# Hybrid trunk on one core: kept weights moved among the pooled branch's products, and the pool's first banks taken from other pairs

## The chip, the core and the metric

One Trainium2 chip, one core of it. The metric is the device time of one execution in microseconds; the figure for a kernel is the median over its runs. Within a trace, times count from the first instruction (the span), and the profiled execution's own time is the span and what lies around it.

## The reference, cut to what matters

```python
D_MODEL = 1024; SEQ = 1024; N_META = 16; DEPTH = 1; D_FF = 2816; HGRN_HEADS = 4; CHUNK = 64
...
h = jnp.concatenate([meta, x], axis=1)                      # 1040 rows
u = rmsnorm(h, mix_norm_pre[l])
proj = u @ w_in[l]
q, f_logit, i_in, g_out, v_pool, gate_a, gate_b = jnp.split(proj, cuts, axis=-1)
a = hgrn2(q, f_logit, i_in, g_out, lbs[l], hgrn_out_norm[l])      # 4 heads, chunked recurrence
p = multiscale_pool(v_pool, pool_proj[l], pool_scale[l])
z = (jax.nn.sigmoid(gate_a.astype(jnp.float32)) * (a @ w_branch_hgrn[l])
     + jax.nn.sigmoid(gate_b.astype(jnp.float32)) * (p @ w_branch_pool[l]))
h = h + rmsnorm(z @ w_out[l], mix_norm_post[l])
u = rmsnorm(h, ffn_norm_pre[l])
gt = causal_dwconv(u @ ffn_w_gate[l], ffn_conv_w[l], ffn_conv_b[l])
y = (jax.nn.gelu(gt, approximate=True) * (u @ ffn_w_up[l])) @ ffn_w_down[l]
h = h + rmsnorm(y, ffn_norm_post[l])
```

Matrices are float32. The kernel makes three products of each: an operand is split into a high part (a cast) and a low part (operand minus high part), and high*high, high*low and low*high are added up in PSUM.

## The kernel before, in words

The trunk runs as a row of stages on TensorE (PE). Up to 326 us of the span come the norm, the projections and the gates; the gates' products are made by Strassen's seven-product scheme in a PSUM pool of four pairs of banks ("pf"). Then the pool "ps" of eight single banks is opened, and the stage that the change is about runs from 326 to 567 us. From there come the output projection (w_out, tile names pm) and the feed-forward part with its own Strassen products.

**The order of the middle stage.** A string, ORDER, names the steps, and PE runs them in just that order (`manual_schedule` holds PE alone). The other engines' instructions are put in order by the framework's scheduler from the order of writing; each engine then runs its own list strictly in order. The words of the string:

- `hN` is the next step of head N of the recurrence. A step has pieces on several engines: k and q are scaled on VectorE (DVE, L676, L682), a level of scores goes to PE (tile `sl`, L693 or L699), masked copies follow on DVE (L714), copies on ScalarE (ACT, L708, L746), transposes, state updates (`ds`, `st`), the output (`po` on PE, L794, L795 on ACT), its norm (`ms` on PE, L803 and L804 on ACT with table loads) and its product with the gate.
- `PVpN` to `PVsN` are the quarters of the pooled branch's projection out of w_in, `spN` the pooling itself, `G` the output gate, `PPN` the pool's own projection of one group (nine matmuls, tile `ppp`), evicted by ACT (L842) and DVE (L843).
- `BBaN`, `BBbN` are the halves of the pooled branch's product for 128 output columns (tile `pbb`), `BAaN`, `BAbN` and `BAN` those of the recurrent branch (tile `pba`), 36 matmuls each. Their weights come two products at a time through `wsplit2`: a load into a buffer `wraw` (L162), ACT's cast into `whi` (L163), DVE's subtraction into `wlo` (L164). Their results are multiplied on DVE with a gate (L881) that is read back from DRAM (L877, transfer `sa<-sscr`), and the two branches are added (L1189).
- `saN` splits a head's output for the BA products (L835 on ACT, L836 on DVE: `ah`, `al`).
- `w0` to `w3` call `keep_first`: load a unit of the feed-forward gate's weights (L944), cast it (L924, two casts), subtract (L925, two), and owe four stores of 256 KB to DRAM tensors `kept..` (L939), two of the high part out of a `whi` buffer, two of the low part out of `wraw`. `w4` and `w5` are single steps of `keep_unit` (three and four of them): loads (L951), sums on DVE (L922), casts, subtractions, stores. The feed-forward part reads all `kept..` tensors back after 650 us in place of making the splits itself.

**What ties them together.** The buffers `wraw`, `whi` and `wlo` are three each, taken in turn by branch weights, kept pieces and, later, the splits of w_out (load L1222, ACT's cast L1229, POOL's subtraction L1231). A buffer that holds a kept piece comes free when its store has landed. All loads and stores named here are issued by SyncE (SP), in one list, in order; `pay()` writes the owed stores behind the next finished product.

**The banks.** `proj_parts` (L194) allots three banks to a product of three column chunks and, before, hands them out in reverse: the first chunk goes to the bank allotted last. The pool "ps" begins on the eight banks that "pf" just gave back; the first PV product took banks 6, 7 and 0, its first chunk bank 0, which is half of the pair that the last gate product was evicted from (L862).

Of the kernel before, what the change touches and what calls it, by code (L numbers as in the profile page):

```python
# [54 lines left out]

ORDER = ("h0 h1 PVp0 PVq0 h0 PVr0 h1 PVs0 h0 PVp1 h1 PVq1 h0 PVr1 h1 PVs1 h0 sp0 PVp2 h1 PVq2 h0 sp1 PVr2 h1 PVs2 "
# [4 lines left out]
POOLED = ()  # L61
VLOAD = 8
TRUNC = False
# [6 lines left out]
def trunk_kernel(ctx: ExitStack, tc: tile.TileContext, x, meta_tokens, mix_norm_pre,  # L70
# [4 lines left out]
    act, dve, pool_e, pe = nc.scalar, nc.vector, nc.gpsimd, nc.tensor  # L75
# [8 lines left out]
    def open_pool(key, bufs, space=bass.MemoryType.SB):  # L84
        stage[key] = ExitStack()
        cnt[0] += 1
        stage[key, "p"] = stage[key].enter_context(
            tc.tile_pool(name=f"{key}{cnt[0]}", bufs=bufs, space=space, reuse_waits="tile"))

    def close_pool(*keys):  # L90
        for key in keys:
            stage[key].close()
# [3 lines left out]
    def nm(s):  # L96
        cnt[0] += 1
        return f"{s}_{cnt[0]}"
# [7 lines left out]
    def bank(name="ps"):  # L106
        return stage["ps", "p"].tile([P, 512], F32, tag="ps", name=nm(name))
# [39 lines left out]
    def wsplit(src, n_k, n_c, eng=dve):  # L147
        raw = wst.tile([P, n_k * n_c], F32, tag="wraw", name=nm("wraw"), bufs=NRAW, padded_shape=[P, 1024])
        with tc.issue_after(stage["after"].ins) if "after" in stage else nullcontext():
            stage["load"] = nc.sync.dma_start(raw.rearrange("p (k c) -> p k c", k=n_k), src)  # L150
        hi = wst.tile([P, n_k * n_c], F32R, tag="whi", name=nm("whi"), padded_shape=[P, 1024])
        lo = wst.tile([P, n_k * n_c], F32R, tag="wlo", name=nm("wlo"), padded_shape=[P, 1024])
        act.copy(hi, raw)
        eng.tensor_tensor(lo, raw, rr(hi), ALU.subtract)
        return [(hi.rearrange("p (k c) -> p k c", k=n_k), lo.rearrange("p (k c) -> p k c", k=n_k))]
# [11 lines left out]
    class Loader:  # L167
# [10 lines left out]
        def next(self):  # L178
            self.at += 1
            return self.got[self.at - 1]  # L180

    def wblock(w, k0, n_k, c0, n_c):
        return w[k0 * P : (k0 + n_k) * P, c0 : c0 + n_c].rearrange("(k p) c -> p k c", p=P)

    def mm3(ps, a, b, first, last):
        (ahi, alo), (bhi, blo) = a, b
        pe.matmul(ps, ahi, bhi, start=first, stop=False)  # L187
        pe.matmul(ps, ahi, blo, start=False, stop=False)  # L188
        pe.matmul(ps, alo, bhi, start=False, stop=last)  # L189

    def proj(*a, **k):
        for banks in proj_parts(*a, **k):
            pass
        return banks  # L194

    def proj_parts(w, col, n_k, xs, chunks, ws=None, name="pj", by_bank=0, cuts=()):

        if ws is None:
            ws, = wsplit(wblock(w, 0, n_k, col, P), n_k, P)
        whi, wlo = ws  # L200
        banks = [bank(name) for _ in chunks][::-1]
        for k in range(n_k - by_bank):
            if k in cuts:
                yield banks
            for (lo, n), ps in zip(chunks, banks):
                xhi, xlo = xs(k, lo, n)
                pe.matmul(ps[:, :n], whi[:, k, :], xhi, start=(k == 0), stop=False)  # L207
                pe.matmul(ps[:, :n], whi[:, k, :], xlo, start=False, stop=False)  # L208
            for (lo, n), ps in zip(chunks, banks):
                xhi, _ = xs(k, lo, n)  # L210
                pe.matmul(ps[:, :n], wlo[:, k, :], xhi, start=False, stop=(k == n_k - 1))  # L211
        for (lo, n), ps in zip(chunks, banks):
            for k in range(n_k - by_bank, n_k):
                mm3(ps[:, :n], (whi[:, k, :], wlo[:, k, :]), xs(k, lo, n), False, k == n_k - 1)
        yield banks
# [812 lines left out]
    with tc.manual_schedule(engines={E.Activation, E.DVE, E.PE}):  # L1028
# [59 lines left out]
        for h in range(EARLY_G):  # L1088
            src, n_k, xs, chunks, post = job("G", h)
# [24 lines left out]
    gates.finish()  # L1114
    close_pool("pf")
    open_pool("ps", 8, PSUM)

    jobs_ = [(k.rstrip("ap"), i) for k, i in order if k[0].isupper() and k[-1] not in "bqrs"]
    branch = [o_ for o_ in jobs_ if o_[0] in ("BA", "BB")]
# [21 lines left out]
    with tc.manual_schedule(engines={E.PE}):  # L1141
        for kind, i in order:
# [17 lines left out]
            src, n_k, xs, chunks, post = job(kind, i)  # L1160
# [3 lines left out]
            if part in "bs":  # L1164
                banks = next(halves_of[kind, i])
# [12 lines left out]
            if part in "ap":  # L1178
# [4 lines left out]
            banks = proj(None, 0, n_k, xs, chunks, ws=ws, name="p" + kind.lower(),  # L1183
                         by_bank=2 if (kind, i) == ("BA", KD - 1) else 0)
# [390 lines left out]
    with tc.manual_schedule(engines={E.PE, E.Activation, E.DVE, E.Pool}):  # L1575
        for i in (1, "m", 0):
            R[i] = Row(0 if i == "m" else HALO + i * P, HALO if i == "m" else P, pair("pm"))
        for c in range(3):
            for at in range(KD - LAST):
                first_, _, then_ = SEAM[c][at].rpartition("|")  # L1580
# [130 lines left out]
    with tc.manual_schedule(engines={E.Activation, E.DVE}):  # L1711
        for s_ in range(3):
            banks = [[bank("pd") for _ in range(NT)] for _ in range(2)]
# [24 lines left out]
    banks = [bank("pd") for _ in range(NT)]  # L1738
# [74 lines left out]
```

## Time and profile before

| | |
|---|---|
| runs | 1319.77, 1320.24, 2585.35 us; median 1320.24 |
| the profiled execution | 1320.58 us, of which 1318.9 are the span |
| mean granted TensorE clock | 0.993 of full speed |
| DMA traffic | 247.62 MB, mean 188 GB/s |

The first number to look at is how much of the span PE is idle, then where. The rows that the argument rests on stand in the prediction. A row of the waits names an engine and line, the operation that released it, and "us in total, times, longest". A row of the windows gives for one stretch its length, the busy time of PE, of PE's weight loads, DVE, ACT and POOL, each with its count of instructions, then PEclk (the granted clock), the busy share of the 16 DMA engines, and GB/s. A row of the chain has start, duration and what ran. In a timeline the brackets at a row's end give the idle time ahead of it and what ended it.

### The profile page before, as it was taken

Reading aid. Unit: us, or ns where it says so; the run is one execution under the profiler, and the core shown is the slowest. Engines: PE = TensorE matmul, PEld = TensorE weight load, DVE = VectorE, ACT = ScalarE, POOL = GpSimd, SP = SyncE. Lnnn points to the kernel's source line nnn. Section 1 sums busy time; section 2 is a strip of 40 time slices with the busy share of each in tenths; the row PEclk is TensorE's granted clock in tenths of the full one; section 3 lists DMA queues with packets and bytes.
Section 4 is the critical chain, followed back from the end, with each engine's and each line's share of the span. In section 5 each row is a group of like instructions: output and inputs, shape, how many; then the busy total and the mean of one; then the engine's idle time right before and its main releaser. Section 6 shows DMA issues by size and latency. Waiting matters only on the chain.

```text
span 1318.9 us, 21954 instructions
## 1 busy us (share of the span) xinstructions
PE 1292.7 (98%) x8650; PEld 1140.0 (86%) x8650; DVE 956.6 (73%) x1293; ACT 524.6 (40%) x905; POOL 353.3 (27%) x307
## 2 busy tenths in 40 slices
PE   8999999999999999799999999999999999999997
PEld 7799899998999899767898888888888888888886
DVE  6768965454876767655588999888998985455758
ACT  5554533332245536235564322222332323444443
POOL 3015333220000000060035555554655642000000
PEclk9999999999999999899999999999999999999999
DMA  8135642325523546887677777667777799666644
GB/s 274 42 105 174 194 157 104 110 99 162 151 85 127 167 144 229 293 298 268 240 256 255 186 207 185 179 199 191 166 170 162 162 244 310 208 223 224 226 173 160
DMA packets 143801, 247.62 MB, mean 188 GB/s; under 512 B 11000, under 2 KB 75164, under 8 KB 143698
## 3 DMA queue, kind: packets, MB, share of 16 engines
q1 hardware_dynamic: 127026, 213.42, 48.2%
q0 software_dynamic: 12064, 24.38, 11.2%
q10 hardware_dynamic: 4608, 8.41, 1.7%
q8 instruction: 68, 1.11, 0.3%
q14 instruction: 35, 0.29, 0.1%
HBM read 174.11 MB, written 95.09 MB: 204 GB/s over the span
## 4 chain that ended last, share of the span: by engine, by line
PE 91%; DMA 3%; DVE 2%; POOL 1%; ACT 1%; issue 1%; SPq 0%; DVEq 0%; POOLq 0%; ACTq 0%
PE P L307 17%; PE P L308 17%; PE P L310 17%; PE pd L187 5%; PE pd L188 5%; PE pd L189 5%; PE pm L188 2%; PE pm L189 2%; PE pm L187 2%; PE ppv L207 1%; PE pbb L207 1%; POOL wlo L1231 1%; PE pv L188 1%; PE ppv L211 1%; PE pv L187 1%; PE ppv L208 1%
## 5 line engine op out<-in xcount | busy, mean ns | idle before, releaser
L308 PE MATMUL P<-v,whi 128*128 128x512 f32 (+2 forms) x408 | 140.7, 353 | 0.0
L307 PE MATMUL P<-v,whi 128*128 128x512 f32 (+2 forms) x408 | 140.7, 352 | 0.0
L310 PE MATMUL P<-v,wlo 128*128 128x512 f32 (+2 forms) x424 | 135.1, 349 | 0.0
L278 POOL TENSOR_TENSOR swa<-wraw,wraw 128x512 f32<-128x512 f32 x32 | 48.7, 1521 | 191.3 <-DMA wraw<-in_ffn_w_gate_dram 73.3
L252 ACT CAST whi<-wraw 128x512 fp32r<-128x512 f32 x90 | 53.1, 618 | 102.1 <-PE P L308 87.3
L1523 DVE TENSOR_TENSOR rot<-wraw,rot 128x1024 fp32r<-128x1024 f32 x31 | 38.0, 1224 | 72.3 <-ACT rot L1522 72.2
L307 PEld LDWEIGHTS P<-v,whi 128*128 128x128 f32 x408 | 76.7, 188 | 10.5
L308 PEld LDWEIGHTS P<-v,whi 128*128 128x128 f32 x408 | 76.6, 188 | 10.2
L310 PEld LDWEIGHTS P<-v,wlo 128*128 128x128 f32 x424 | 74.0, 188 | 10.8
L188 PE MATMUL pd<-rot 128*128 128x512 f32 x274 | 82.5, 388 | 0.0
L189 PE MATMUL pd<-rot 128*128 128x512 f32 x274 | 82.5, 388 | 0.0
L187 PE MATMUL pd<-rot 128*128 128x512 f32 x274 | 81.9, 388 | 0.1
L253 DVE TENSOR_TENSOR wlo<-wraw,whi 128x512 fp32r<-128x512 f32 x86 | 75.5, 901 | 2.7 <-ACT whi L252 2.7
L252 ACT CAST whi<-swa 128x512 fp32r<-128x512 f32 x64 | 38.1, 619 | 90.9 <-PE P L308 80.7
L253 DVE TENSOR_TENSOR wlo<-swb,whi 128x512 fp32r<-128x512 f32 x64 | 65.5, 1032 | 8.8 <-ACT whi L252 8.7
L1522 ACT CAST rot<-wraw 128x1024 fp32r<-128x1024 f32 x31 | 32.7, 1054 | 90.8 <-PE pd L189 89.4
L307 PE MATMUL P<-uhi,whi 128*128 128x258 f32 (+2 forms) x240 | 68.5, 303 | 0.0
L308 PE MATMUL P<-ulo,whi 128*128 128x258 f32 (+2 forms) x240 | 68.4, 303 | 0.0
L1451 DVE SCALAR_TENSOR_TENSOR y<-g,par,y 128x1024 f32<-128x1024 f32 x44 | 65.6, 1491 | 0.8
L252 ACT CAST whi<-swb 128x512 fp32r<-128x512 f32 x64 | 38.1, 618 | 69.6 <-PE P L308 57.9
L307 PE MATMUL P<-t4h,whi 128*128 128x258 f32 (+2 forms) x228 | 65.5, 304 | 0.0
L308 PE MATMUL P<-t4l,whi 128*128 128x258 f32 (+2 forms) x228 | 65.4, 304 | 0.0
(387 smaller groups left out, 3836.1 us busy)
## 6 DMA issues: line engine op xcount, KB each, us to landing
wraw<-in_w_in_dram SPq DMA_DIRECT2D x36, 512.0 KB, 4.7
yt<-ysum SPq DMA_DIRECT2D x33, 512.0 KB, 5.9
wraw<-in_ffn_w_gate_dram SPq DMA_DIRECT2D x26, 512.0 KB, 6.6
wraw<-in_ffn_w_up_dram SPq DMA_DIRECT2D x22, 512.0 KB, 6.3
wsum<-in_ffn_w_down_dram SPq DMA_DIRECT2D x22, 512.0 KB, 8.7
wraw<-in_w_out_dram SPq DMA_DIRECT2D x18, 512.0 KB, 4.3
ysum<-ys SPq DMA_DIRECT2D x11, 768.0 KB, 5.3
sa<-sscr SPq DMA_DIRECT2D x16, 513.0 KB, 5.9
```

Of the source, the lines that this page charges most:

```text
L187: pe.matmul(ps, ahi, bhi, start=first, stop=False)
L188: pe.matmul(ps, ahi, blo, start=False, stop=False)
L189: pe.matmul(ps, alo, bhi, start=False, stop=last)
L252: act.copy(hi, src)
L253: (pool_e if 4 <= i < 2 * self.early else dve).tensor_tensor(lo, src, rr(hi), ALU.subtract)
L278: pool_e.tensor_tensor(s1, a21, a22, ALU.add)
L307: pe.matmul(d, whi[:, k, :], xh[:, c : c + w], start=(k == 0 and onto is None), stop=False, **go)
L308: pe.matmul(d, whi[:, k, :], xl[:, c : c + w], start=False, stop=False, **go)
L310: pe.matmul(x[:, o : o + w], wlo[:, k, :], xh[:, c : c + w], start=False, stop=(k == 3), **go)
L1451: dve.scalar_tensor_tensor(a, g[:, j : j + SEQ], cvw[:, j, m : m + 1], a, ALU.mult, ALU.add)
L1522: act.copy(hi, src)
L1523: dve.tensor_tensor(lo, src, rr(hi), ALU.subtract)
```

## The change

Three edits.

1. **ORDER.** `w0` to `w3` leave their places among BBa4, BBa5, BA2 and BA3 and stand behind BBb0, BBb1, BBb2 and BBb3. The three `w4` follow from BBb4 to BBb5, the four `w5` from BBb6 to BAb0; no `w` stands behind BAb0 any more. And `PP2 PP3 h3` becomes `PP2 h3 PP3`.
2. **Bank order.** `proj_parts` hands out its three banks in the order in which they were allotted. This holds for every product that goes through it.
3. **Three spare banks.** Behind `open_pool("ps")` three banks are allotted and one column of each is set to zero by DVE; they are not used otherwise. The first PV product then gets banks 5, 4 and 3 and not 6, 7 and 0.

```diff
-         "Gr3 h2 h1 Gs3 h3 PP1 h2 PP2 PP3 h3 BBa0 h2 BBb0 h3 BBa1 h2 BBb1 h3 BBa2 h2 BBb2 h3 BBa3 h2 h3 BBb3 h2 h3 "
...
+         "Gr3 h2 h1 Gs3 h3 PP1 h2 PP2 h3 PP3 BBa0 h2 BBb0 h3 w0 BBa1 h2 BBb1 h3 w1 BBa2 h2 BBb2 h3 w2 BBa3 h2 h3 "
...
-        banks = [bank(name) for _ in chunks][::-1]
+        banks = [bank(name) for _ in chunks]
...
     open_pool("ps", 8, PSUM)
+    for spare in [bank("spare") for _ in range(3)]:
+        dve.memset(spare[:, :1], 0.0)
```

Code behind the third edit stands two lines lower, so that L1229 of before is L1231 after it. The numbers at the end of tile names differ between the two programs; they only tell tiles apart.

PE at the end of the pool's projection, before: `ppp_4913` to `ppp_4911` are PP2's three chunks, `ppp_4931` to `ppp_4929` PP3's, `sl_4954` a level of head 3.

```order
L211 MATMUL ppp_4912<-plh_4194,wlo_4702 128x342
L211 MATMUL ppp_4911<-plh_4194,wlo_4702 128x342
L207 MATMUL ppp_4931<-plh_4383,whi_4707 128x342
L208 MATMUL ppp_4931<-pll_4384,whi_4707 128x342
L207 MATMUL ppp_4930<-plh_4383,whi_4707 128x342
...
L211 MATMUL ppp_4929<-plh_4383,wlo_4708 128x342
L699 MATMUL sl_4954<-q_4514,k_4512 32x16 x32
L207 MATMUL pbb_4995<-uhi_88,whi_4858 128x342
```

And after, the same place, with `sl_4935` for head 3 and `ppp_4972` for PP3's first chunk:

```order
L211 MATMUL ppp_4918<-plh_4200,wlo_4708 128x342
L211 MATMUL ppp_4919<-plh_4200,wlo_4708 128x342
L699 MATMUL sl_4935<-q_4520,k_4518 32x16 x32
L207 MATMUL ppp_4972<-plh_4389,whi_4713 128x342
L208 MATMUL ppp_4972<-pll_4390,whi_4713 128x342
L207 MATMUL ppp_4973<-plh_4389,whi_4713 128x342
...
L211 MATMUL ppp_4974<-plh_4389,wlo_4714 128x342
L207 MATMUL pbb_4999<-uhi_88,whi_4864 128x342
```

Head 3's level has moved ahead of PP3, and PP3 takes its chunks in the order of their allotment.

ACT from PP3's evictions (L842) to the middle of the BB products, before: `whi_5185` are the weights of BB4 and BB5, `whi_5390` those of BB6 and BB7, the L740, L746, L708 and L755 rows belong to heads 2 and 3.

```order
L842 ACTIVATE uhi_88<-ppp_4929,par 128x342
L163 CAST whi_5185<-wraw_5184 128x1024
L740 COPY scm_4442<-sm_5014 16x2
L746 COPY sc_4440<-near_4441 32x8x32 x4
L708 COPY sc_4440<-sl_5144 32x8x32 x2
L163 CAST whi_5390<-wraw_5389 128x1024
L740 COPY scm_4646<-sm_5194 16x2
L746 COPY sc_4644<-near_4645 32x8x32 x4
L708 COPY sc_4440<-sl_5262 64x8x64
L708 COPY sc_4644<-sl_5296 32x8x32 x2
L755 COPY kt_5341<-pt_5342 128x512
```

And after: `whi_5129`, `whi_5258` and `whi_5348` are the kept pieces of w0, w1 and w2, `whi_5198` and `whi_5425` the same branch weights as above.

```order
L924 CAST whi_5129<-wraw_5127 128x512 x2
L842 ACTIVATE uhi_88<-ppp_4972,par 128x342
...
L163 CAST whi_5198<-wraw_5197 128x1024
L746 COPY sc_4446<-near_4447 32x8x32 x4
L708 COPY sc_4446<-sl_5157 32x8x32 x2
L924 CAST whi_5258<-wraw_5256 128x512 x2
L740 COPY scm_4652<-sm_5211 16x2
L924 CAST whi_5348<-wraw_5346 128x512 x2
L746 COPY sc_4650<-near_4651 32x8x32 x4
L708 COPY sc_4446<-sl_5286 64x8x64
L163 CAST whi_5425<-wraw_5424 128x1024
L708 COPY sc_4650<-sl_5324 32x8x32 x2
```

w0's casts now stand ahead of PP3's evictions, and those of w1 and w2 between the heads' copies. With three `whi` buffers in turn, `whi_5198` takes the buffer of w0's piece and `whi_5425` that of w2's, each of which is free once its two stores have landed.

ACT ahead of the last BA products, before: `zc` are splits of finished rows of z, `whi_5996` and `whi_6061` hold w2 and w3, `whi_6043` the weights of BA6 and BA7, `whi_6292` the first of w_out.

```order
L924 CAST whi_5931<-wlo_5932 128x512 x2
L924 CAST whi_5990<-wraw_5853 128x512
L1130 CAST zc_6207<-sa_5797 128x256
...
L924 CAST whi_5996<-wraw_5994 128x512 x2
L163 CAST whi_6043<-wraw_6042 128x1024
L924 CAST whi_6061<-wraw_6059 128x512 x2
L1130 CAST zc_6361<-sa_6066 128x256
L1134 CAST zc_6361<-sa_6066 128x2
L1229 CAST whi_6292<-wraw_6290 128x1024
```

And after, where `whi_6066` are BA6's and BA7's and `whi_5951` is the last piece of w5:

```order
L163 CAST whi_5937<-wraw_5936 128x1024
L1132 CAST zc_6213<-sa_5868 128x256
L1136 CAST zc_6213<-sa_5868 128x2
L924 CAST whi_5951<-wraw_5764 128x512
L1132 CAST zc_6218<-sa_5891 128x256
...
L163 CAST whi_6066<-wraw_6065 128x1024
L1231 CAST whi_6298<-wraw_6296 128x1024
L1132 CAST zc_6228<-sa_6024 128x256
```

No kept piece is left around the cast for BA6 and BA7. Before, that cast took the `whi` buffer of a w5 piece (`whi_5931`, which leaves by the stores kept8h and kept9h); after, it takes the one of the weights of BA2 and BA3, free when PE has read them. On SP the stores of the kept pieces move up with their casts, and the loads of w_out come to stand right behind the last gate load and ahead of the loads of the norms' gains.

4 rows, old and new, of the table ORDER are left out of this document.

## The prediction

> **What bounds the kernel.** I read the page's engine shares first, then PE's waits, then the stage by windows, then the chain of work at the places where PE waits.
>
> ```profile
> PE 1292.7 (98%) x8650; PEld 1140.0 (86%) x8650; DVE 956.6 (73%) x1293; ACT 524.6 (40%) x905; POOL 353.3 (27%) x307
> PE pba L207 <- ACT whi L163: 8.5, 1, 8.5
> PE pm L188 <- POOL wlo L1231: 3.2, 3, 1.7
> PE ppp L207 <- DVE uhi L843: 1.2, 1, 1.2
> PE ppv L207 <- DVE sg L862: 0.9, 1, 0.9
> PE pba L208 <- DVE al L836: 0.8, 1, 0.8
> PE ppp L207 <- DVE near L714: 0.3, 1, 0.3
> PE pba L207 <- DVE sa L881: 0.3, 1, 0.3
> ```
>
> PE bounds: 98% of the span. The change neither adds nor takes away a matmul, so all it can win is PE's idle time, and the time in which PE runs at a lower clock. Of these waits one, 8.5 us in front of the product BA6, is larger than the others together. The windows say the same, and show the clock (second last but two columns: PEclk, DMA share, GB/s):
>
> ```profile
> 420.00:440.00 20.00, 18.46 (x402) 16.48 (x389) 17.16 (x31) 16.83 (x28) 0.00 (x0) 0.95 0.73 230
> 440.00:510.00 70.00, 70.00 (x719) 67.11 (x717) 48.42 (x91) 32.21 (x56) 0.00 (x0) 0.99 0.45 146
> 510.00:568.00 58.00, 47.69 (x284) 46.26 (x283) 42.21 (x71) 16.87 (x31) 1.46 (x1) 0.91 0.81 280
> 438.00:442.00 4.00, 4.00 (x76) 3.73 (x71) 4.00 (x9) 1.99 (x4) 0.00 (x0) 0.58 1.01 311
> 554.00:558.00 4.00, 4.00 (x16) 3.76 (x16) 2.78 (x4) 1.14 (x2) 0.00 (x0) 0.57 0.98 333
> ```
>
> In 440 to 510, where the change puts w0 to w3 and w4, PE has no idle time and the DMA engines are less than half busy; in 510 to 568, where they come from, PE stands 10.3 us (58.00 less 47.69) at a DMA share of 0.81. The chain through the long wait:
>
> ```profile
> 540.10 7.25 DMA sa<-sscr
> 547.44 1.35 DVE sa L881 x3
> ...
> 552.56 1.05 ACT whi L163
> 553.66 0.65 PE pba L207
> ...
> 561.51 4.96 DMA kept4l<-wraw
> 566.54 2.37 POOL wlo L1231
> 568.95 0.50 PE pm L188
> 542.95 1.45 SPq L939 DMA_DIRECT2D kept8h<-whi  x1
> DMA to landing us min/median/max: 2.0/3.6/8.2
> ```
>
> PE waits for ACT's cast of BA6's weights, and the cast for something that ended about 552.5. The chain names DVE's L881, but this cast reads nothing of it. What it does need, by the program, is the store kept8h out of the buffer that it writes into; that store was issued at 542.95 for 1.45 us (the SP timeline), and stores of this stretch took up to 8.2 us to land (the kept stores from 510 to 568): 544.4 + 8.2 = 552.6. So the long wait is a kept piece that leaves a `whi` buffer too slowly on a full DMA. And the w_out stage waits at 568.95 for POOL, whose first split waited for w3's store kept4l.
>
> **The change part by part.**
>
> *A, the pool's first banks.* The first PV chunk no longer waits for the last gate product's eviction but for the one before.
>
> ```profile
> L862 DVE TENSOR_TENSOR sg<-p,P x2: 689/690/690, 323.2 to 325.4; 128x512 f32<-128x512 f32 x1, 128x514 f32<-128x514 f32 x1
> 543.46 0.15 DVE L1135 TENSOR_TENSOR zc<-sa,zc 128x2 fp32r<-128x2 f32 x1
> ```
>
> That one began at 323.2 and took 0.69, so its banks were free at 323.9; PE was held until the later one (325.4 + 0.69 = 326.1) for 0.9 us. The wait goes whole: -0.9. The three memsets are new on DVE. No row shows one on DVE; the nearest is the smallest operation on that queue, 0.15 us for 128x2 (L1135), so at most 0.5 together, behind the last eviction. Ends 0 and +0.5; I take 0, since the first product's weights and operands are split by then and PE reads nothing that stands behind the memsets at once.
>
> *B, PP2, h3, PP3 and w0 beside them.*
>
> ```profile
> 436.00 0.43 PE L207 MATMUL ppp<-plh,whi 128*128 128x342 f32 x1 [1.16 <-DVE uhi L843]
> 437.86 1.01 PE L699 MATMUL sl<-q,k 128*32 128x16 f32 x64
> 437.64 1.42 ACT L842 ACTIVATE uhi<-ppp,par 128x342 fp32r<-128x342 f32 x3 [0.48 <-PE ppp L211]
> 442.57 0.56 DVE L843 SCALAR_TENSOR_TENSOR uhi<-ppp,par,uhi 128x342 fp32r<-128x342 f32 x1
> 431.49 2.06 SPq L162 DMA_DIRECT2D wraw<-in_w_branch_pool_dram  x2
> DMA to landing us min/median/max: 5.2/6.2/7.3
> L925 DVE TENSOR_TENSOR wraw<-wraw,whi 128x512 fp32r<-128x512 f32 x4 | 2.7, 685 | 0.3 <-ACT whi L924 0.3
> 443.87 0.36 PE pbb L207
> ```
>
> PP3 waits 1.2 + 0.3 us for banks that DVE evicts. Head 3's level, 1.0 us, now lies ahead of PP3 and can fill that. But DVE is busy all the time here (17.16 of 20 us), so PP3's banks come no sooner, and the two BBa0 chunks behind wait for evictions in their turn, which now have head 3's scaling between them. Against it, w0 is new here: its load stands on SP where BB4's stood, which left at 431.5, and such loads (L944) landed after 5.2 to 7.3 us, so 436.7 to 438.8, and its two casts (about 1.2 us) stand ahead of PP3's evictions on ACT, its two subtractions (2 x 0.69 = 1.4) ahead of them on DVE. PP3's last eviction, which ended at 443.1, moves to about 444.5; BBb0, which began at 443.9, needs it for its second half, about 1.5 us in, at 445.3. Covered, with a margin of about 1 us; w0's cast is what covers or uncovers it, and each us that the load is later than that PE pays. Ends: -2.2 (0.5 us of bank waits and the 1.7 us of clock, see below, if the stretch falls together well) and +2.6 (the whole 1.4 of DVE plus 1.2 of ACT on PE). The hidden case is the nearest by the rows; I take 0.
>
> *The clock there.* In 438 to 442 PE ran at 0.58, which cost 0.42 x 4 = 1.7 us; the only idle time ahead of it is 1.2 and 0.3 us. I leave it as it is. [...]
>
> *C, kept pieces among the heads and at BAa0 to BAb0.* ACT gets w1, w2, w3 (two casts each) and the w4 steps between the heads' copies. The casts themselves cost ACT 1.2 us a piece in a stretch where it works 32.21 of 70 us, DVE 48.42 of 70. Work as such is hidden. What is not sure is the order: ACT and DVE stop at a cast whose buffer has not been stored yet, and the heads' copies queue behind it. This row shows such a stop in the kernel before, and one further on:
>
> ```profile
> ACT whi L163 <- DMA kept0l<-wraw: 3.7, 1, 3.7
> 522.38 1.14 ACT L924 CAST whi<-wraw 128x512 fp32r<-128x512 f32 x2 [6.19 <-DMA kept7h<-whi]
> 448.00:456.00 8.00, 8.00 (x141) 7.51 (x140) 5.19 (x12) 1.92 (x4) 0.00 (x0) 1.00 0.01 2
> 473.12 0.87 PE pt L754 x8
> 495.86 0.16 PE pbb L207
> 496.00:504.00 8.00, 8.00 (x53) 8.00 (x52) 6.86 (x10) 7.89 (x10) 0.00 (x0) 1.00 0.76 264
> ```
>
> The stop of 3.7 us cost PE nothing. After the change three weight casts wait for stores in this way: BB4's (for w0), BB6's (for w2), BA0's (for a w4 piece). The first two fall where the DMA is nearly empty (0.01 from 448 to 456), so a store takes about the 2.0 us that is the minimum above; BB4 begins at about 474 (behind the `pt` at 473.1) and BB6 at 495.9, both some 20 us later. The third falls near 496 to 504, where ACT works 7.89 of 8 us, in the norm of head 3, on which BAb0 waited 0.8 us (`al`) already, and BAa1 0.3. There I expect about 1 us more. Ends: -1.1 (both old waits go) and +8.2 (a store of the slowest landing stands on PE in full). I take +1, nearer to the stop that cost nothing.
>
> *D, BA6's weights.* No kept piece is left near this cast. Its buffer is now free when PE has read the weights of BA2 and BA3, its load waits for the last w5 piece, which stands behind BAb0, and 4.5 products of 36 matmuls of 0.16 us (the row at 495.86), 26 us, lie between. -8.5. With the idle time the half clock behind it goes: 0.43 x 4 = 1.7 in 554 to 558, and 0.2 for the 0.34 us from 553.66 on at the same rate: -1.9. What would be late next is the gate read-back of BA4 (`sa<-sscr`, 7.25 us); it was issued at 540.1 behind kept stores, and now stands ahead of the last four of them.
>
> *E, the start of w_out.* Its first splits waited for w3's store. Those buffers now belong to pieces that are gone by then, and the loads start behind the last gate load. The first wait, 1.7, goes; two more of 1.6 together (3.2 less 1.7) belong to POOL's pace (2.4 us a split) and I leave them. Ends -3.2 and 0.
>
> Sum: -0.9 + 0 + 1.0 - 8.5 - 1.9 - 1.7 = -12.0. The profiled execution took 1320.6 (its span is 1318.9): 1308.6. The median of the runs is 0.3 below that execution, so the forecast is **1308**.
>
> **The rivals.**
>
> *Slower than before: stores hold ACT in the BB products.* Between 440 and 510 there is now a row of casts in one ring of three `whi` buffers: w0, BB4, w1, w2, BB6, w3, w4. Each link is load, cast, store, next cast, and the heads' copies queue behind. If four of the links (w0 to w3) each hold ACT longer than the heads can bear, PE stands four times. A stop of 3.7 us was free, so it decides where a stop reaches 3.7 + 12.0 / 4 = 6.7 us; the 6.19 of the row above would just not do, and at the slowest landing, 8.2, PE loses 4 x 4.5 = 18 and the kernel ends at 1308 + 18, or **1326**. For it: the same ring caused the 8.5 us before, and the stores that w0 to w3 add fill just this empty DMA. Against it: 6 MB at most come into a stretch that has room for twice what it moves (0.45 busy).
>
> *Half is given back.* The stop comes once or twice, at w0's load or at BA0's cast, where ACT has no room: one store of 8.2 us on PE in place of my 1.0 gives 1308 + 7.2, or **1315**. For it: 7.89 of 8 us on ACT; against it: 5 us of traffic fewer lie ahead of that store.
>
> *Everything comes.* The clock at 438 stays up, both waits at BAa1 and BAb0 go, and w_out does not wait: 1308 - 2.2 - 2.1 - 1.5, or **1302**.
>
> *The change doesn't do what it says.* The long wait would stay if another kept piece or the late gate loads held BA4 to BA6: only A and E come, 1320.2 - 2.6, or **1318**. Against it: by the program that cast waits for no store any more.
>
> **How the numbers follow.** The forecast with its own range of 1303 to 1312: 0.57. Half given back, 1312 to 1318: 0.18. Everything, under 1303: 0.07. Long wait stays, 1317 to 1320: 0.05. Slower than before, over 1320: 0.13. The range of 1301 to 1319 leaves out the last and some of the edges, under 2 in 10. A measurement of this kernel tells about 2% from no change, and 2% is 26 us: only a slower rival at over 1346 (0.02) lies above, and nothing priced reaches 1294 (0.01). So same: 0.97.
>
> **What the profile after would show.** A: no wait of `ppv` for L862. B: `sl` in the gap ahead of PP3 and BBa0 starting within 1 us of 438 (less 0.9); wrong if BBb0 waits for `uhi`. C: no PE wait from 445 to 495; one of 1 to 2 us at BAa1 or BAb0; wrong if `sl`, `pt` or `po` wait. D: no PE wait for L163, PEclk 1.00 from 510 on, DMA share well below 0.81 there. E: `pm` waits of at most 1.6. What would make it wrong most: an ACT wait for a kept store over 4 us with a PE wait behind it.

## The result and the profile after

| | before | after |
|---|---|---|
| median (lowest to highest) | 1319.77 us (from 1317.94; one run of 2585.35 stands outside the comparison) | 1311.21 us (1309.09 to 1312.50) |
| ratio after / before | | 0.9937, 95% interval 0.9922 to 0.9953 |
| the profiled execution (its span) | 1320.58 us (1318.9) | 1311.92 us (1310.2) |
| mean granted TensorE clock | 0.993 | 0.996 |

The change won 8.6 us between the medians, 0.63% by the ratio. That is within 2%, as forecast, and some 3 us less than the forecast's sum. The page's engine shares of the kernel after, and the largest of PE's waits for this stretch (us in total, times, longest):

```profile
PE 1291.0 (99%) x8650; PEld 1139.6 (87%) x8650; DVE 963.7 (74%) x1296; ACT 524.4 (40%) x905; POOL 355.4 (27%) x307
PE pba L208 <- DVE al L836: 3.2, 2, 1.8
```

PE's timeline after, the rows from 430 to 565 ahead of which PE stood idle (in brackets; "issue" means that the profile shows nothing that ended the wait):

```profile
434.61 0.73 PE L699 MATMUL sl<-q,k 128*32 128x16 f32 x64 [1.43 <-issue]
438.98 0.42 PE L207 MATMUL pbb<-uhi,whi 128*128 128x342 f32 x1 [1.35 <-DVE uhi L843]
440.05 0.40 PE L207 MATMUL pbb<-uhi,whi 128*128 128x342 f32 x1 [0.49 <-DVE near L714]
507.79 0.42 PE L801 MATMUL ms<-rh,onesr 128*128 128x342 f32 x1 [0.72 <-DVE sa L881]
518.47 0.43 PE L208 MATMUL pba<-al,whi 128*128 128x342 f32 x1 [1.38 <-DVE al L836]
521.94 0.42 PE L208 MATMUL pba<-al,whi 128*128 128x342 f32 x1 [1.80 <-DVE al L836]
562.60 0.47 PE L187 MATMUL pm<-whi,zc 128*128 128x512 f32 x1 [0.70 <-DVE sa L881]
```

The wait of 8.5 us for ACT's L163, those of 3.2 for POOL and the 0.9 of `ppv` are gone. Smaller ones, which were not there before or were smaller, stand in three places: around PP3 and BBa0, 1.43 ahead of head 3's level (`sl`), where `ppp` had waited 1.16 and 0.32, and on top of it 1.35 and 0.49 for `pbb`, together 3.27 in place of 1.48; `ms` 0.72 in head 3's norm and `al` 1.38 and 1.80 (0.8 before) in the BA products that read it; and `pm` 0.70 at the start of w_out, for another releaser than before. Between 526 and 562, where the long wait was, nothing is left. PE's idle time, span less busy, fell from 1318.9 - 1292.7 = 26.2 us to 1310.2 - 1291.0 = 19.2.

Where the time went by stages is read best from the first and last start of three tiles, which stand in the middle of each row ("first to last"). First before:

```profile
L207 PE MATMUL ppv<-uhi,whi x96: 317/322/431, 326.2 to 384.9; 128*128 128x346 f32 x64, 128*128 128x348 f32 x32
L207 PE MATMUL pba<-ah,whi x90: 313/323/652, 509.0 to 563.3; 128*128 128x342 f32 x90
L187 PE MATMUL pm<-whi,zc x128: 388/389/500, 566.9 to 670.3; 128*128 128x512 f32 x128
```

And after:

```profile
L207 PE MATMUL ppv<-uhi,whi x96: 317/322/431, 325.2 to 383.8; 128*128 128x346 f32 x64, 128*128 128x348 f32 x32
L207 PE MATMUL pba<-ah,whi x90: 316/320/488, 511.0 to 558.1; 128*128 128x342 f32 x90
L187 PE MATMUL pm<-whi,zc x128: 389/389/500, 562.6 to 661.9; 128*128 128x512 f32 x128
```

| stretch | before | after | change |
|---|---|---|---|
| to the first PV product | 326.2 | 325.2 | -1.0 |
| first PV to the first BA product | 182.8 | 185.8 | +3.0 |
| first BA to the first w_out product | 57.9 | 51.6 | -6.3 |
| w_out, first to last | 103.4 | 99.3 | -4.1 |

Together -8.4, of the 8.7 by which the spans differ. So the stretch ahead of the first BA product, into which the kept pieces moved, became longer by 3.0, and the BA stretch that they left gained 6.3 rather than the 9.4 of the forecast (-8.5 - 1.9 + 1.0). The 3.0 belongs to this one execution: in a second one of the same kernel ("after, once more" below) that stretch takes 184.0, which is +1.2.

Three windows of these places after (columns as before):

```profile
440.00:446.00 6.00, 5.95 (x90) 5.70 (x91) 4.98 (x10) 0.34 (x2) 0.00 (x0) 0.72 0.89 316
522.00:526.00 4.00, 4.00 (x16) 4.00 (x17) 3.88 (x8) 0.62 (x1) 0.00 (x0) 0.57 0.83 204
545.00:562.00 17.00, 16.91 (x108) 16.62 (x106) 11.87 (x19) 1.72 (x4) 4.26 (x4) 1.00 0.76 246
```

The half clock at 554 is gone with the idle time ahead of it, but 522 to 526 now has one that costs the same: 0.43 x 4 = 1.7 us.

What stands behind the two waits for `al` is in the timeline of ACT, in the middle of head 3's norm; first before, then after:

```profile
494.11 0.59 ACT L794 COPY o<-po 128x512 f32<-128x512 f32 x1 [1.82 <-PE po L792]
494.59 1.14 ACT L924 CAST whi<-wlo 128x512 fp32r<-128x512 f32 x2
495.90 0.59 ACT L794 COPY o<-po 128x512 f32<-128x512 f32 x1 [0.17 <-PE po L792]
```

```profile
495.00 0.59 ACT L794 COPY o<-po 128x512 f32<-128x512 f32 x1 [1.82 <-PE po L792]
498.25 1.14 ACT L924 CAST whi<-wraw 128x512 fp32r<-128x512 f32 x2 [2.66 <-DMA kept7h<-whi]
499.30 0.58 ACT L794 COPY o<-po 128x512 f32<-128x512 f32 x1
```

Before, 1.8 us lie between the two copies of `o`, after it 4.3. The cast of a kept piece stands between them in both. Before, it is w4's first and does not wait. After, it is w5's first, and it stops for 2.66 us, until the store kept7h has landed, which empties the `whi` buffer of w4's last piece. The second copy waits behind it, though its own input is long there. The chain of work carries the 2.5 us on to PE:

```profile
493.17 4.98 DMA kept7h<-whi
...
498.25 1.14 ACT whi L924 x2
499.39 0.49 ACT o L794
...
517.19 1.22 DVE al L836
...
520.75 1.15 DVE al L836
521.94 0.42 PE pba L208
```

### The profile page after: what moved, and what is told of

The parts are those of the page before. It is cut to its first block, busy times and chain, and to the rows that moved or that the text cites. A ratio compares the mean times of both kernels' runs of the same rounds, so it can differ in the third digit from the quotient of the medians.

```text
span 1310.2 us, 21958 instructions
## 1 busy us (share of the span) xinstructions
PE 1291.0 (99%) x8650; PEld 1139.6 (87%) x8650; DVE 963.7 (74%) x1296; ACT 524.4 (40%) x905; POOL 355.4 (27%) x307
## 4 chain that ended last, share of the span: by engine, by line
PE 95%; ACT 2%; DVE 2%; DMA 1%; issue 1%; SPq 0%; DVEq 0%; ACTq 0%
PE P L307 17%; PE P L308 17%; PE P L310 17%; PE pd L187 5%; PE pd L189 5%; PE pd L188 5%; PE pm L187 2%; PE pm L188 2%; PE pm L189 2%; PE ppv L207 1%; PE ppv L211 1%; PE ppv L208 1%; PE pv L188 1%; PE pv L187 1%; PE pv L189 1%; PE pg L207 1%
## 5 line engine op out<-in xcount | busy, mean ns | idle before, releaser
L252 ACT CAST whi<-swb 128x512 fp32r<-128x512 f32 x64 | 38.1, 618 | 70.8 <-PE P L308 57.9
L307 PE MATMUL P<-t2h,whi 128*128 128x258 f32 (+2 forms) x228 | 65.3, 304 | 0.1
```

The costliest lines, as they stand in the source:

```text
L252: act.copy(hi, src)
L307: pe.matmul(d, whi[:, k, :], xh[:, c : c + w], start=(k == 0 and onto is None), stop=False, **go)
```

## The experiments

Every kernel was timed beside the kernel before on the same chip, in four to eleven runs. The theory to be tested: the long wait was one kept store in the buffer of BA6's cast (D); what was given back lies in one place, a store ahead of w5's first cast, in the middle of head 3's norm. The rivals: the gain comes from the emptier DMA as such; what was given back comes from PP3 and head 3 changing places; or from the row of casts in the BB products. The table tells how they came out, the sections why.

| kernel | median, us | ratio to before (95%) |
|---|---|---|
| after | 1311.21 | 0.9937 (0.9922 to 0.9953) |
| banks alone | 1318.51 | 0.9996 (0.9987 to 1.0004) |
| after, PP3 ahead of head 3 | 1309.63 | 0.9930 (0.9917 to 0.9942) |
| after, w5's casts held | 1307.88 | 0.9914 (0.9902 to 0.9926) |
| after, w2 and w3 late | 1310.07 | 0.9931 (0.9917 to 0.9944) |
| after, w4 and w5 late | 1310.17 | 0.9929 (0.9916 to 0.9943) |
| held, PP3 ahead of head 3 | 1308.31 | 0.9916 (0.9903 to 0.9930) |
| after, w0 to w3 in one place | 1315.76 | 0.9969 (0.9956 to 0.9982) |
| held, w2 and w3 late | 1311.10 | 0.9933 (0.9921 to 0.9946) |
| before, w2 one place later | 1314.58 | 0.9966 (0.9954 to 0.9979) |
| before, w2 two places earlier | 1316.70 | 0.9982 (0.9973 to 0.9991) |
| after, once more | 1311.17 | 0.9945 (0.9931 to 0.9959) |
| after, w5's casts held, once more | 1307.69 | 0.9914 (0.9900 to 0.9927) |

### The banks alone

The kernel after with the ORDER of before: only edits 2 and 3 are left.

> The old ORDER with the bank order and the three spare banks of the change. If step A stands alone: the 0.9 us wait of ppv for L862 is gone, everything behind it comes 0.9 to 1.1 us earlier, the 8.5 us wait in front of BA6 stays, and the time is 1318.9 (1319.8 less 0.9). Rival: the order in which a product's chunks take their banks moves other waits too (PP3's 1.2 + 0.3, BAa1's 0.3); then the waits of ppp and pba change by more than 0.5 us in sum and the time leaves 1318.5 to 1319.3.

1318.51 us, no change that can be measured: by the interval between 1.7 us won and 0.5 lost. PE's `ppv` wait is gone, as after. BA6 waits still, 6.9 us; why it is not the 8.5 that was expected stays open. So nearly all of the 8.6 us is ORDER's.

### After, with PP3 ahead of head 3 again

```diff
-PP1 h2 PP2 h3 PP3 BBa0 h2 BBb0 h3 w0
+PP1 h2 PP2 PP3 h3 BBa0 h2 BBb0 h3 w0
```

> The changed kernel with PP2 PP3 h3 again in place of PP2 h3 PP3; w0 stays behind BBb0. Theory: the swap alone cost the time at BBa0, since head 3's L676 and L682 (2 x 0.6 us) went ahead of PP2's and PP3's evictions on DVE and BBa0's banks wait for those (1.35 + 0.49 us). Then those two waits go, PP3's 1.2 + 0.3 come back, BBb0 begins 1 to 2 us earlier than at 444.7, and the time is 1 to 2 us under the changed kernel's 1311.2, at 1309.2 to 1310.2. Rival: w0's casts and subtractions ahead of PP3's evictions cost it; then BBa0 or BBb0 still wait for L843 and the time stays at 1311.

1309.63 us. The wait of 1.43 ahead of `sl` and the two of `pbb` (1.35 + 0.49) go, and three ahead of PP3 (1.08, 0.26, 0.32) come back, with 0.24 at a later `sl`: 1.9 us in place of 3.27. So the swap brings the waits at BBa0, and in the profiled executions it costs PE some 1.4 us of waits. The time lies in the range that went with this, and the medians differ by 1.6, but the intervals overlap, so the times don't tell the cost apart. The two `al` waits stay, 3.2 together, so the swap is not what cost the 2.4 us at `al`. And behind these two waits the clock stays at 1.00 here:

```profile
522.00:526.00 4.00, 4.00 (x26) 4.00 (x27) 4.00 (x8) 0.82 (x2) 0.00 (x0) 1.00 0.81 237
```

### After, with w5's casts held behind head 3's norm

```diff
+        stage["rh"] = stage["split"]
...
-        act.copy(hi, src)
+        stage["split"] = act.copy(hi, src)
...
-            act.copy(hi, src)
+            with tc.issue_after(stage["rh"].ins) if what[0][0][0] == UP0 else nullcontext():
+                act.copy(hi, src)
```

All of w5's casts are put on ACT's queue behind the cast of the head's `rs`. That takes the stopped cast from between the two copies of `o`, and also the next piece's two casts of 0.6 us each, which stood inside the norm that follows (508.95 and 512.17 in the kernel after, none of them up to 512 here).

> The changed kernel with w5's casts ordered behind the cast of head 3's squares (L835) on ACT. Theory: in the changed kernel head 3's second output copy (L794) stood behind w5's first cast, which waited 2.7 us for the store kept7h, and the head's norm, its split (al) and BAa0 to BAb0 came late by that. Then L794 runs 2 us or more earlier than at 499.3, the waits of ms (0.72) and of pba for al (1.38 + 1.80) fall under 1.2 us in sum, the half clock at 522 to 526 goes with them, and the time is 1306 to 1308.5. Rival: ACT has too much work from 496 to 515 in any order (four table loads, two norms); then the waits for al stay over 2 us in sum and the time stays at 1310 to 1312.

1307.88 us, and 1307.69 in the repeat at the end of this chapter: 3.4 us less than after, and better than both kernels of the case. Of the ten runs of the two held kernels the slowest took 1309.53 us, of the ten of after (the repeat below among them) the fastest 1309.09. In the ACT timeline of this kernel the copies follow each other as before the change, and the cast comes behind:

```profile
496.40 0.59 ACT L794 COPY o<-po 128x512 f32<-128x512 f32 x1 [1.20 <-PE po L792]
...
498.11 1.06 ACT L836 CAST rh<-rs 128x1026 fp32r<-128x1026 f32 x1
499.07 1.13 ACT L926 CAST whi<-wraw 128x512 fp32r<-128x512 f32 x2
```

Of PE's waits, `ms` is gone and one `al` is left (the code is a line lower here):

```profile
PE pba L208 <- DVE al L837: 1.1, 1, 1.1
```

With 1.1 us of idle time in place of 3.2 the clock stays at 1.00 from 518 to 530. So w5's casts ahead of the norm's end, of which the first stopped for 2.66 us, are shown to be the place where the change gave time back: 0.7 (`ms`) + 2.1 (`al`) make 2.8 of the 3.4, and the 1.7 of clock, which is not lost in every execution, covers the rest.

### After, with w2 and w3 back behind BA2 and BA3

```diff
-h3 w2 BBa3 h2 h3 BBb3 h2 h3 w3 BBa4
+h3 BBa3 h2 h3 BBb3 h2 h3 BBa4
...
-BA2 BA3 BA4
+BA2 w2 BA3 w3 BA4
```

> The changed kernel with w2 and w3 back behind BA2 and BA3; w0, w1, w4 and w5 stay early. Their 3 MB go back into the stretch of the BA products, but the cast of BA6's weights now takes a buffer that PE frees, not a store. Theory (the 8.5 us were a buffer held by a kept piece's store): BA6 waits 2 us at most, w_out's splits wait again for w3's store by 1 to 3 us, the time is 1311 to 1315. Rival (the 8.5 us were the full DMA): BA6 or its neighbours wait 5 us or more for weights or gates, the time is 1316 to 1320.

1310.07 us: not slower than after, a miss for both theories, which had some waits come back. The window of the stretch in question in this kernel:

```profile
545.00:562.00 17.00, 17.00 (x107) 16.70 (x106) 14.31 (x20) 3.83 (x6) 6.95 (x5) 1.00 1.00 380
```

The DMA engines are as full as in the kernel before (1.00 here, 1.04 there in the same window), and PE does not stand at all. So it was not the full DMA that held BA6. With w4 and w5 early, the buffer that BA6's cast takes holds no kept piece on its way out, and that is enough.

### After, with w4 and w5 at their old places

```diff
-BBb4 h2 h3 w4 BBa5 w4 BBb5 h3 w4 BBa6 h2 sa0 BBb6 sa1 w5 BBa7 h3 w5 BBb7 sa2 w5 BAa0 BAa1 sa3 BAb0 w5 BAb1 BA2 BA3
+BBb4 h2 h3 BBa5 BBb5 h3 BBa6 h2 sa0 BBb6 sa1 w4 BBa7 h3 w4 BBb7 sa2 BAa0 w4 BAa1 sa3 w5 BAb0 w5 BAb1 w5 BA2 w5 BA3
```

> The changed kernel with all w4 and w5 steps back at their places of before (w4 behind BBb6, BBa7, BAa0, w5 behind BAa1 to BA2), w0 to w3 early. BA6's cast then takes the buffer that PE frees with BA5's last matmul, and no kept store. Theory (a kept piece's store held the buffer): the wait in front of BA6 shrinks from 8.5 us to cast plus release, 1 to 3 us; head 3's output copies stand behind no cast that waits for a store, so the waits of ms and al stay under 1.5 us in sum; the time is 1308 to 1311. Rival (the amount of kept traffic beside the BA products): five of the seven w4 and w5 pieces are back there, BA6 waits 5 us or more, the time is 1314 to 1319.

1310.17 us. Here both halves are seen in one kernel: `al` waits 0.8 as before the change, since no w5 cast stands in the norm, and BA6 waits again, but little:

```profile
PE pba L207 <- ACT whi L163: 0.7, 1, 0.7
PE pba L211 <- DVE wlo L164: 0.4, 1, 0.4
```

Moving w0 to w3 alone is thus also enough for D, nearly: either half of the ORDER edit takes at least 7.4 of the 8.5 us, and the two do not add.

### Held, with PP3 ahead of head 3

The edits of the second and the third experiment together.

> The held casts of the third experiment together with PP2 PP3 h3. If the swap costs 1 to 2 us by itself, the time is 1306 to 1307; if the swap is neutral and only the clock at 436 to 444 differs from one execution to the next, it is 1307.9 within 0.8, as with the held casts alone.

1308.31 us, as the held kernel within the intervals: no cost of the swap can be told here either, nor that the two edits depend on each other.

### After, with w0 to w3 all behind BBb0

```diff
-BBb0 h3 w0 BBa1 h2 BBb1 h3 w1 BBa2 h2 BBb2 h3 w2 BBa3 h2 h3 BBb3 h2 h3 w3 BBa4
+BBb0 h3 w0 w1 w2 w3 BBa1 h2 BBb1 h3 BBa2 h2 BBb2 h3 BBa3 h2 h3 BBb3 h2 h3 BBa4
```

This tests the slower rival of the prediction by making its mechanism worse: four links of the ring of `whi` buffers in a row.

> The changed kernel with w0, w1, w2 and w3 all behind BBb0: four kept pieces in a row in one ring of three buffers, each waiting for the store of the one before. Rival of the prediction (stores hold ACT and the heads' copies queue behind): ACT stops for stores four times between 440 and 465, PE waits for sl, pt or BB weights 3 us or more in sum, and the time is 1314 or more. Theory (in the BB products the heads have slack, so stops of up to about 4 us are free there): ACT stops, PE waits less than 1.5 us there, the time is 1310 to 1313.

1315.76 us, 4.6 more than after. ACT stops for stores and then for a load of branch weights, and PE for head work (ACT's waits, ACT's timeline, then PE's):

```profile
ACT whi L924 <- DMA kept1h<-whi: 8.0, 2, 4.0
467.04 1.05 ACT L163 CAST whi<-wraw 128x1024 fp32r<-128x1024 f32 x1 [3.34 <-DMA wraw<-in_w_branch_pool_dram]
```

```profile
469.83 0.66 PE L754 MATMUL pt<-ident,k 128*128 128x128 f32 x4 [1.79 <-DVE sa L881]
471.96 1.85 PE L693 MATMUL sl<-q,k 128*64 128x64 f32 x16 [1.37 <-DVE q L682]
```

The waits of 3.2 us do not follow the two store stops directly. PE stands some 20 us later. In between, ACT's casts of branch weights stop for their loads, 1.24 us until 457.19 and 3.34 until 467.04, and PE then waits for DVE, for its products with the gate (L881) and its scaling (L682). That these loads were late because of the stops, and that DVE's subtraction and the scaling queued behind the late cast, is an estimate from this order of events. The low clock behind the waits (0.97 over the 54 us from 446 to 500, some 1.6 us; the scores at 471.96 take 1.85 us, where they took 1.15 in the kernel after) makes up the rest of the 4.6. So a row of kept pieces in one place does reach PE, by this estimate through late weights. That the stops for stores would do it alone is not shown. In the kernel after, the pieces stand one to each product. ACT stops there for stores too, 3.58 and 1.42 us, and PE waits for nothing behind them.

### Held, with w2 and w3 late

> The held casts together with w2 and w3 behind BA2 and BA3. If only the kept stores ahead of head 3's copies and ahead of BA6's cast matter, w2 and w3 are as good there: 1306 to 1308.5, no PE wait over 1.2 us behind 446. If the DMA at full share in the BA products costs, 1309 or more.

1311.10 us, as in the second case: the two good edits together are worse than the hold alone (1307.88). The `al` wait is 1.1 as in the held kernel, but a new wait stands ahead of w_out:

```profile
560.28 0.47 PE L187 MATMUL pm<-whi,zc 128*128 128x512 f32 x1 [2.71 <-DVE sa L882]
```

What made DVE's product with the gate (L882) late is not shown. The DMA is full here (1.01 from 545 to 562), and ACT works 4.05 of these 17 us and DVE 12.16; a late load of w_out's weights, with the splits of z and the product queued behind its cast, would fit that. In the fourth experiment the same late pieces showed no wait there, but PE came to that place some 3 us later (560.7; here 560.28 less the 2.71). What PE gains ahead of this place it hands back at it.

### Before, with w2 one place later

The most direct test of D: one word of the kernel before is moved, the traffic is the same, and only who takes which `whi` buffer changes.

```diff
-"w5 BAb1 w5 BA2 w5 w2 BA3 w3 BA4 BA5 BA6 BA7"
+"w5 BAb1 w5 BA2 w5 BA3 w2 w3 BA4 BA5 BA6 BA7"
```

> The kernel before with one word moved: w2 stands behind BA3 (beside w3) and no longer behind the last w5 ahead of BA3. The kept traffic beside the BA products stays as it was; but the ring of whi buffers turns by one, and the cast of BA6's weights takes the buffer that PE frees with BA5, not the one that the store kept8h holds. Theory (the store in the buffer): the wait in front of BA6 falls from 8.5 us to under 3, the half clock behind it goes; w_out's first splits, which now wait for w2's and w3's stores, may give back 1 to 4 us; the time is 1311 to 1316. Rival (the full DMA): BA6 waits 5 us or more and the time stays at 1317 to 1320.

1314.58 us: 4.5 us for one word. BA6's wait falls from 8.5 to 0.7 (and 0.4 for its `wlo`), with the DMA as full as before (1.00, 1.04 there):

```profile
545.00:562.00 17.00, 12.76 (x76) 11.61 (x74) 11.60 (x19) 4.71 (x8) 1.99 (x1) 1.00 1.00 369
546.03 0.42 PE L207 MATMUL pba<-ah,whi 128*128 128x342 f32 x1 [0.67 <-ACT whi L163]
...
559.99 0.49 PE L187 MATMUL pm<-whi,zc 128*128 128x512 f32 x1 [1.65 <-DVE sa L881]
563.48 0.79 PE L188 MATMUL pm<-wlo,zc 128*128 128x512 f32 x1 [3.00 <-POOL wlo L1231]
```

The second part of the rows is what the late pieces cost: w_out now waits 1.65 us for DVE and 3.00 for POOL's split.

### Before, with w2 two places earlier

```diff
-"w5 BAb1 w5 BA2 w5 w2 BA3 w3 BA4 BA5 BA6 BA7"
+"w5 BAb1 w2 w5 BA2 w5 BA3 w3 BA4 BA5 BA6 BA7"
```

> The kernel before with w2 two steps earlier, ahead of the last two w5. The traffic stays in this stretch, BA6's cast again takes a buffer that PE frees (with BA5), but the w5 cast ahead of it on ACT waits for w2's stores, which land in up to 8.2 us here. Theory: the wait in front of BA6 is 1 to 4 us, and the time 1310 to 1315. Rival (the full DMA): 5 us or more, 1317 to 1320.

1316.70 us, between the ranges of both. The cast of the high parts of BA6's weights is early, and PE waits for it 1.9 in place of 8.5. But behind it now come waits that the long one had hidden (PE's timeline, then DVE's):

```profile
547.10 0.42 PE L207 MATMUL pba<-ah,whi 128*128 128x342 f32 x1 [1.91 <-ACT whi L163]
549.16 0.65 PE L207 MATMUL pba<-ah,whi 128*128 128x342 f32 x1 [1.17 <-DVE sa L881]
553.87 1.22 PE L211 MATMUL pba<-ah,wlo 128*128 128x342 f32 x3 [3.77 <-DVE wlo L164]
```

```profile
548.60 1.35 DVE L881 TENSOR_TENSOR sa<-sa,pba 128x342 f32<-128x342 f32 x3 [3.69 <-DMA sa<-sscr]
```

DVE stops 3.69 us for the gate read-back of an earlier product, and the subtraction that makes BA6's `wlo` stands behind that on its queue. Together 1.9 + 1.2 + 3.8 = 6.9 us, nearly as long as the wait in the kernel before. So the rival, a late gate on a full DMA, is half right for this kernel: with the store out of the way, the read-back held PE nearly as long. That it would have done so in the kernel before too, had the store not held BA6, is likely but not shown: with w2 one place later, the same traffic left waits of 0.7 and 0.4 only. The ORDER of the kernel after has neither wait.

### After, once more

> The changed kernel unchanged, beside the others on the same chip. Theory and rival alike: 0.9937 of the kernel before within 0.0015, and the two waits for al (1.4 and 1.8 us) as before. If the half clock at 440 to 444 or at 522 to 526 is a matter of chance in each execution, the profile shows one of them gone or moved while the waits stay.

1311.17 us. The waits at BBa0 (1.35 and 0.48) and for `al` (1.38 and 1.79) are the same. Those around PP3 fall a little otherwise (0.55, 0.54 and 0.32, which with BBa0's makes 3.24). But the clock at BBa0 is another than in the first execution:

```profile
438.00:442.00 4.00, 2.16 (x13) 1.87 (x13) 4.00 (x10) 1.75 (x4) 0.00 (x0) 1.00 0.83 222
```

1.00, and from 442 to 446 as well, where it was 0.72 over 440 to 446. At 522 to 526 it is low again (0.66).

### Held, once more

> The kernel with the held casts once more, to tell whether it stands below the changed kernel (0.9937 and 0.9945 of the kernel before) or was a lucky sample at 0.9914. Theory (the casts ahead of head 3's copy cost 3 us): 0.9905 to 0.9925, the waits of ms and of pba for al under 1.2 us in sum. Rival (chance): 0.993 or more.

1307.69 us, with no `ms` wait and `al` at 1.0: the gain of the hold is confirmed.

## Why the prediction was near, and where it was off

The forecast was 1308 with a range of 1301 to 1319; it came to 1311.2. The likeliest case had its own range to 1312 and holds the result, near its upper end. By the sum's terms, from the stages and waits of the two profiled executions above (that these terms and the four stages both add up to -8.4 is in part luck, since the waits leave some 0.4 us of two stages unexplained, with opposite signs):

| term | predicted | measured |
|---|---|---|
| A, the first banks | -0.9 | -1.0 |
| B, PP3 and w0 | 0 | +1.9 |
| C, kept pieces among the heads and BAa0 to BAb0 | +1.0 | +4.5 |
| D, BA6's weights, and the clock behind | -8.5 - 1.9 | -8.5 - 1.9 |
| E, start of w_out | -1.7 | -3.4 |
| sum | -12.0 | -8.4 |

**A** came as said in the trace; the first PV product starts 1.0 earlier. By itself it is too small to be measured.

**B** was put at 0, and its cover did not hold. BBb0 starts 119.5 us behind the first PV product, where it was 117.6 (in the two programs' timelines): +1.9. The cause is not w0's load, which the prediction had as what covers or uncovers PP3's evictions: no row of PE waits for it. Its casts waited for no load at all, but for PP3's matmuls that still read the buffer:

```profile
436.88 1.14 ACT L924 CAST whi<-wraw 128x512 fp32r<-128x512 f32 x2 [0.74 <-PE ppp L208]
```

It is the other thing that the prediction names and then leaves unpriced: the BBa0 chunks wait for evictions in their turn, with head 3's scaling now between them on DVE. The timeline of DVE shows it, L676 and L682 on both sides of the eviction L843:

```profile
437.74 0.70 DVE L676 TENSOR_TENSOR k<-k,f 128x528 f32<-128x528 f32 x1
438.36 0.56 DVE L843 SCALAR_TENSOR_TENSOR uhi<-ppp,par,uhi 128x342 fp32r<-128x342 f32 x1
439.02 0.68 DVE L682 TENSOR_TENSOR q<-q,f 128x512 f32<-128x512 f32 x1
```

These two waits (1.35 and 0.49) came on top, and the kernel with PP3 ahead of head 3 has neither. The old ones did not go: head 3's level was to fill PP3's 1.16 and 0.32, but PE stood 1.43 us ahead of that level itself, for something that the profile does not show. In all PE stands 3.27 us here, where it was 1.48, and the clock cost 1.7 in both executions (0.42 x 4 before, 0.28 x 6 after). So of the +1.9, 1.8 are idle time. In the median of the runs this cost is not told from nothing.

**C** is the step that was off most: the mechanism was right, the size and the cast were not. Predicted was about 1 us at `al`, "nearer to the stop that cost nothing". Measured: `ms` 0.7 that is new, `al` 3.2 against 0.8, less 0.3 for BAa1's wait that went, and 1.7 for the half clock behind these waits: +4.5. The prediction looked for the stop at BA0's cast, for a w4 piece. The piece was right: the store that held ACT is that of w4's last. But BA0's cast (490.22) waited for no store; the stop came two casts later, at w5's first piece, between the two copies of `o` in the norm, where ACT has no slack up to BAb0 (busy 11.88 of the 12 us from 500 to 512). The prediction also left the clock out of the price of a stop, though the 1.7 is chance: the same two waits for `al` stand in the kernel with PP3 ahead of head 3 and in the one with w0 to w3 in one place, and there the clock stayed at 1.00 behind them. The hold recovers 3.4 and shows the cause. The rival "half is given back" had this mechanism, with 8.2 in place of the 2.66 that the stop took, and was thus dearer than what came.

**D** came as worked out. The wait is gone and PE's clock is 1.00 from 526 to 562. That a store in the buffer held it, and not the traffic, is shown by the kernels with a full DMA and no long wait (w2 and w3 late; w2 one place later). The trace of before says it as well: ahead of the cast ACT's queue stands 7.7 us at one semaphore, from 544.8 to 552.5, which the landing of kept8h ends, while the chain named DVE's L881. In the source view of L163 it is the longest of the row (in ns), with the start of the last:

```profile
L163 ACTq EVENT_SEMAPHORE  x11: 17/38/7707, 431.9 to 544.8; - x11
```

What the prediction called "late next", the gate read-back, came in one kernel, w2 two places earlier. Two details differ: the DMA share from 510 on was to be well below 0.81 and is 0.72, and the clock was to be 1.00 there and is 0.97, because of the half clock at 522.

```profile
510.00:568.00 58.00, 54.12 (x320) 51.95 (x319) 44.13 (x65) 19.11 (x33) 10.35 (x7) 0.97 0.72 239
```

**E** was left at the first of three waits, the other 1.6 us put down to POOL's pace. That was wrong: all three went from the list of waits, and more than its end of -3.2 (w_out is 4.1 shorter, less 0.7 for the new wait ahead of it). POOL's pace is the same (2.41 us a split in the median, 2.40 before), but its first splits start early enough for the pace not to matter, the first at 543.00 and the second here:

```profile
551.26 2.38 POOL L1233 TENSOR_TENSOR wlo<-wraw,whi 128x1024 fp32r<-128x1024 f32 x1 [4.64 <-ACT whi L1231]
```

Before, the first started at 566.54. Against the first w_out product its head start was 0.4 us (566.54 to 566.9) and is now 19.6 (543.00 to 562.6). A wait on a pacing engine at the start of a stage is here a matter of that head start.

**The slower rival** did not come; bunching the four pieces shows that kept pieces can hold PE in the BB products (3.2 us of waits), by the estimate there through late weights. **Open**: of the 8.7 us between the spans, 0.3 lie outside the four stages; what head 3's level waited for; B's and C's sizes rest on single executions, of which the second one of the kernel after has no half clock at BBa0; a fourth `whi` buffer, which might take away these stops, was not tried.

## What to carry to other kernels

Work that is off the bottleneck engine was cheap here by its duration and dear by its place: w5's first casts take 1.14 us of ACT, and their stop of 2.66 us came through to PE. Where an in-order engine may stop for a store of the buffer it writes, list what stands behind it on the queue, and put it behind the last operation that the bottleneck waits for. When a profile names a releaser that the waiting instruction does not read, look in the program for what else it needs, the buffer's last store first, and test it by moving one user of the ring by one place. And price a short stop with what may follow it: the wait (here 3.2 us at `al`), and, in some executions only, the clock (1.7 us).

## What the hardware showed that was not expected

The clock fell to 0.50 for some 3.4 us behind idle times of PE much shorter than that, and not each time. Over single microseconds it was 0.63, 0.50, 0.50 and 0.67 from 522 to 526 in the kernel after, and 0.99, 0.50, 0.50, 0.50 and 0.81 from 437 to 442 in the kernel before: 1.7 us lost in each, which takes 3.4 us at 0.50. Ahead of 522 to 526 stand two waits of 1.38 and 1.80 us within 5 us, and the clock was low in both executions of the kernel after (0.57 and 0.66 over 4 us), but 1.00 behind the same waits in the kernel with PP3 ahead of head 3 and in the one with w0 to w3 in one place. Behind the waits of 1.35 and 0.49 us at BBa0 it was 0.72 over 6 us in the one execution of after and 1.00 in the other, with the same waits. In the second execution of the held kernel it was 0.79, 0.50 and 0.86 over the three stretches of 4 us from 434 to 446, which is 3.4 us lost, twice as much. The kernel with the banks alone waits 1.1, 0.3 and 0.3 us ahead of PP3, the kernel before 1.2 and 0.3, and the one has 1.00 where the other had 0.58:

```profile
438.00:442.00 4.00, 3.63 (x60) 2.93 (x62) 4.00 (x9) 1.24 (x3) 0.00 (x0) 1.00 0.94 259
```

What brings such a stretch on, and how long PE must stand for it, is not shown. A single stretch of this kind was worth 1.7 us here (0.43 x 4 from 522 to 526, 0.28 x 6 from 440 to 446 in the kernel after), as much as several terms of the sum above, so differences of that size between two profiled executions say nothing by themselves until the clock has been taken out.
